# A two-layer hybrid decoder block on one core: the mixer's products turned feature-major, and one of four convolution chunks computed on GpSimd

## The chip, the cores and the metric

One core of one Trainium2 chip runs the whole program. The metric is the device time of one execution in microseconds; the time of the kernel before is the median of three executions.

## What is computed

The input is 256 tokens of 1024 features, all in float32, and there are two layers. The part that the change touches is the mixer, one of the four sublayers of a layer:

```python
def hybrid_mixer(u, w_in, b_f, w_attn_out, conv_w, conv_b, g_conv, w_conv_out, w_out):
    z = u @ w_in          # q | k | v | forget logits | conv GLU input | gate_attn | gate_conv
    y_attn = forgetting_attention(q, k, v, f_logit) @ w_attn_out
    y_conv = conformer_conv(z[..., C0:GA0], conv_w, conv_b, g_conv) @ w_conv_out
    merged = sigmoid(z[..., GA0:GC0]) * y_attn + sigmoid(z[..., GC0:]) * y_conv
    return merged @ w_out

def conformer_conv(glu_in, conv_w, conv_b, g_conv):
    a = glu_in[..., :512] * sigmoid(glu_in[..., 512:])
    y = depthwise_causal_conv(a, conv_w)      # 31 taps, 512 channels
    return silu(rmsnorm(y + conv_b, g_conv))
```

Here u is the RMS-normed input. Around the mixer stand, in each layer, a SwiGLU before it and one after it (1024 to 2816 and back) and a small gated embedding step.

## The kernel before, in words

**Products.** Every float32 operand of a product is split into a high and a low part, and each product is three matmuls: high by high, low by high, high by low. Activations are kept feature-major (`xs`, 128 features by 256 tokens for each of 8 chunks). Weights come from HBM in blocks of up to 1 MB into `raw` (3 buffers); ScalarE casts a half block of 1024 columns to `whi`, and VectorE computes `wlo = raw - whi` (6 buffers of each). Two forms of product exist. The feature-major form (`mm_b`) has the weights stationary and the 256 tokens moving, and gives 128 output features by 256 tokens. The token-major form (`mm_a`, used by `block_a`, lines 893 to 905) has 128 tokens stationary and 512 weight columns moving.

**The mixer** (line 908) uses the token-major form for the convolution's input, the values with the forget logits, the two gates, and the two output projections; queries and keys are feature-major (`heads`, line 1066). The root of the RMS norm is a factor for each token. In a token-major result it is one number for each partition, so ScalarE applies it as the `scale` of the tanh (`gate`, line 1187; `conv_in`, line 944). Where a token-major result is needed feature-major, TensorE transposes it: the convolution's input (4 transposes of 128x128 for each half, line 962 onward) and the merged result (16 of them, `turn` in `merged`, line 1220).

**The convolution** (`taps`, line 930) is 31 multiply-adds for each of four chunks of 128 channels by 256 tokens, all on VectorE, each `acc = abuf * w + acc`. They must be done before the norm of the convolution's result (`conv_end`, line 1044), which the products with `w_conv_out` wait for.

**GpSimd** issues a few DMAs, and in each mixer two: the running sum of the forget gates goes to HBM (`ncum`) and comes back spread over all partitions (`fb`). Two selects then put the causal mask into `fb` (`forget`, line 1005). VectorE's first step of every head of the attention reads `fb` (`sc`).

**Order.** All instructions are issued in an order that a planner in the program works out (class `Flow`, and `Weights` for the casts). It keeps a clock for TensorE, VectorE and ScalarE, with a fixed cost for each kind of step, and picks by priority. The taps have priority 4: they fill VectorE's time where a weight half is ready for 1 to 2 halves ahead of TensorE, and come after the next halves that TensorE needs. On the chip each engine runs its list strictly in that order. Nearly every instruction goes through the helper at line 304, so the profile gives L304 for it and groups are told apart by tile names.

Of the kernel before, what the change touches and what calls it, by code (L numbers as in the profile page):

```python
# [8 lines left out]
F32 = mybir.dt.float32  # L9
# [8 lines left out]
P = 128  # L18
T = 256
# [26 lines left out]
GAPS = 31, 62  # L46
# [405 lines left out]
def trunk(ctx: ExitStack, tc: tile.TileContext, x, p, g_ff1, w_ff1_in, w_ff1_out, g_mix, w_in, b_f,  # L452
# [3 lines left out]
    tensor, vector, scalar = (Pinned(tc, e) for e in (nc.tensor, nc.vector, nc.scalar))  # L456
# [52 lines left out]
    def a_blocks(src, kn, c0):  # L509
        order.extend(((src, k0, 4, c0, 512), None) for k0 in range(0, kn, 4))  # L510

    KPARTS = [(0, 8), (8, 7), (15, 7)]
    for l in range(L):
        W = w_in[l]
        ffn_blocks(w_ff1_in[l], w_ff1_out[l], l == 0)
        a_blocks(W, KD, (C0, C0 + CC))
        order.extend(((W, k0, 4, V0, AW + H), None) for k0 in range(0, KD, 4))
        a_blocks(W, KD, (C0 + 2 * P, C0 + CC + 2 * P))
        order.extend(((W, 0, KD, c, 2 * P), None) for c in (Q0, Q0 + 2 * P, K0, K0 + 2 * P))
        for c in (GA0, GA0 + 512, GC0, GC0 + 512):  # L520
            a_blocks(W, KD, c)
        for w in (w_attn_out[l], w_conv_out[l]):
            for n in range(2):
                a_blocks(w, KC, n * 512)
# [368 lines left out]
    def block_a(src, xs, kn, c0, needs):  # L893

        banks = [flow.take(mms) for _ in range(TT)]
        for k0 in range(0, kn, 4):
            blk = wts.take(src, k0, 4, c0, 512)
            for tt in range(TT):
                for h in blk.halves:
                    piece(mm_a_, MA, [(blk, k, (banks[tt].t, xs[k0 + k], tt), (k0 + k == 0, k0 + k == kn - 1))  # L900
                                      for k in range(h.a, h.b)], [needs[k0 + k] for k in range(h.a, h.b)])
            wts.release(blk)
        return banks

    def mm_a_(ps, xs, tt, w, start, stop):
        mm_a(ps, xs, tt, w, start, stop)

    def mixer(l, norm, nxt):
        W = w_in[l]
        norm.root()  # L910
        with tc.tile_pool(name="mixer", bufs=1) as ph, tc.tile_pool(name="attn", bufs=2) as at:
# [9 lines left out]
            scaled = {}  # L921

            def scales():
                yield norm.tok
                for name, f in (("half", 0.5),):
                    scaled[name] = small.tile([P, TT], F32, name=f"r{name}")
                    yield V, vc(TT), lambda: vector.tensor_scalar(out=scaled[name], in0=norm.rtok, scalar1=f, scalar2=None, op0=ALU.mult)
            have_scales = spawn(scales(), prio=0)

            def taps(cc):  # L930
                for t in range(TAPS):
                    for c in cc:
# [9 lines left out]
                        yield V, vc(T, 1), go  # L942

            def conv_in(banks, cc):

                yield have_scales
                rh = scaled["half"]
                avs = []
                for tt in range(TT):
                    sg = yield t1s  # L950
                    av = yield t2s
                    yield A, ac(T, 1), lambda: scalar.activation(out=sg.t[:, :T], in_=banks[tt].t[:, T:], func=AF.Tanh, scale=rh[:, tt:tt + 1])
                    yield A, ac(T, 1), lambda: scalar.activation(out=av.t[:, :T], in_=banks[tt].t[:, :T], func=AF.Copy, scale=rh[:, tt:tt + 1])
                    banks[tt].free()
                    yield V, vc(T), lambda: vector.scalar_tensor_tensor(out=av.t[:, :T], in0=sg.t[:, :T], scalar=1.0, in1=av.t[:, :T],
                                                                        op0=ALU.add, op1=ALU.mult)
                    sg.free()
                    avs.append(av)
                xp = yield xps
                pt = xp.t.rearrange("p (c t) -> p c t", c=2)  # L960

                def go():
                    for tt, av in enumerate(avs):
                        for i in range(2):
                            tensor.transpose(out=pt[:, i, tt * P:(tt + 1) * P], in_=av.t[:, i * P:(i + 1) * P], identity=ident)
                yield PE, 430, go
                for av in avs:
                    av.free()
                yield A, ac(2 * T), lambda: scalar.copy(out=abuf[:, cc[0]:cc[1] + 1, TAPS - 1:], in_=pt)
                xp.free()  # L970
# [3 lines left out]
            banks = block_a(W, norm.xs, KD, (C0, C0 + CC), norm.ready)  # L974
            in0 = spawn(conv_in(banks, (0, 1)))
# [29 lines left out]
            def forget():  # L1005
# [23 lines left out]
                nc.gpsimd.dma_start(out=rows, in_=ncum)  # L1029
                nc.gpsimd.dma_start(out=fb[1], in_=rows.partition_broadcast(P))  # L1030
                for dst, src in ((fb[0], fb[1][:, :, :P]), (fb[1][:, :, P:], fb[1][:, :, P:])):
                    nc.gpsimd.affine_select(out=dst, in_=src, pattern=[[0, H], [-1, P]], compare_op=ALU.is_ge, fill=NEG, base=0,
                                            channel_multiplier=1)
                have_f.at = flow.now + 16000
            spawn(forget(), prio=2)

            banks = block_a(W, norm.xs, KD, (C0 + 2 * P, C0 + CC + 2 * P), norm.ready)
            in1 = spawn(conv_in(banks, (2, 3)))
# [27 lines left out]
            def heads(c0, dst, scale):  # L1066
                evs = []
                for mm in range(AW // (2 * P)):
                    bank = flow.take(mms)
                    blk = wts.take(W, 0, KD, c0 + mm * 2 * P, 2 * P)  # L1070
                    for m in range(2):
                        for h in blk.halves:
                            ks = range(h.a, h.b)
                            piece(mm_b, MB, items_b(blk, bank, m, 0, ks, KD, norm.xs), [norm.ready[k] for k in ks])
                    wts.release(blk)
# [109 lines left out]
            sig = ph.tile([P, 2, TT, D], F32, name="sig")  # L1185

            def gate(banks, gi, cols):
                rh = scaled["half"]
                for tt in range(TT):
                    yield A, ac(512, 1), lambda: scalar.activation(out=sig[:, gi, tt, cols], in_=banks[tt].t, func=AF.Tanh, scale=rh[:, tt:tt + 1])  # L1190
                    banks[tt].free()
            gated = []
            for i in range(4):
                gi, n = divmod(i, 2)
                banks = block_a(W, norm.xs, KD, (GA0, GC0)[gi] + n * 512, norm.ready)
                gated.append(spawn(gate(banks, gi, slice(n * 512, (n + 1) * 512))))
# [11 lines left out]
            def ya_in(banks, n):  # L1208
                cols = slice(n * 512, (n + 1) * 512)
                yield gated[n]  # L1210
                for tt in range(TT):
                    yield V, vc(512), lambda: vector.scalar_tensor_tensor(out=sig[:, 0, tt, cols], in0=sig[:, 0, tt, cols], scalar=1.0, in1=banks[tt].t,
                                                                          op0=ALU.add, op1=ALU.mult)
                    banks[tt].free()
            have_ya = []
            for n in range(2):
                banks = block_a(w_attn_out[l], os_, KC, n * 512, os_ready)
                have_ya.append(spawn(ya_in(banks, n)))

            def merged(bank, n, tt):  # L1220
                cols = slice(n * 512, (n + 1) * 512)
                kk = slice(n * 4, n * 4 + 4)
                yield gated[2 + n]
                yield have_ya[n]
                m2 = yield t2s
                yield V, vc(512, 1), lambda: vector.scalar_tensor_tensor(out=m2.t, in0=sig[:, 1, tt, cols], scalar=1.0, in1=bank.t,
                                                                         op0=ALU.add, op1=ALU.mult)
                bank.free()
                yield V, vc(512), lambda: vector.tensor_tensor(out=m2.t, in0=m2.t, in1=sig[:, 0, tt, cols], op=ALU.add)
                xp = yield xps  # L1230
# [8 lines left out]
                xp.free()  # L1239

# [194 lines left out]
```

## Time and profile before

| | |
|---|---|
| median of three executions | 1121.93 us (1121.37 to 1122.11) |
| the profiled execution, its own time | 1121.54 us |
| its span, first to last instruction | 1119.5 us |
| TensorE busy | 1110.0 us (99%) |
| VectorE busy | 830.3 us (74%) |
| ScalarE busy | 600.4 us (54%) |
| GpSimd busy | 24.7 us (2%) |

The profile is one execution taken by the hardware profiler. Busy time of TensorE is that of overlapping matmuls, so the pace of its work is read from the start times of successive instructions, not from their lengths. Times in the trace count from the start of the span. The first mixer runs from about 195.5 to 331 us and the second from about 744 to 880 us.

### The profile page before, as it was taken

To read this page: it belongs to the slowest core of one execution; us is meant where nothing else is said; L and a number is where in the kernel's file an instruction comes from. 1 tells how busy PE (TensorE), PEld (TensorE's weight loads), DVE (VectorE), ACT (ScalarE), POOL (GpSimd) and SP (SyncE) were. 2 spreads that over 40 slices of the span, in tenths; PEclk is the share of its full clock that TensorE was granted. 3 is DMA by queue.
4 is the path that set the end of the run, shared out by engine and by line. 5 is a ranking of instruction groups with operands and counts; after the bars stand their busy time and mean duration, and the time that the engine had idled before them with its cause. 6 is when DMAs were issued, how large, how long until landed. Compare 5 with 4: busy or idle time off the path is not lost.

```text
span 1119.5 us, 21305 instructions
## 1 busy us (share of the span) xinstructions
PE 1110.0 (99%) x8900; PEld 1065.2 (95%) x8900; DVE 830.3 (74%) x1296; ACT 600.4 (54%) x874; POOL 24.7 (2%) x27
## 2 busy tenths in 40 slices
PE   9999999999999999999999999999999999999997
PEld 9999999897789999999999999999878999999996
DVE  7766656899997866656896665569999887665665
ACT  6544454558555544444654444457576555444454
POOL 1000000030000000000000000000200000000000
PEclk9999999999999999999999999999999999999998
DMA  9755566464457555565467555655535666555541
GB/s 306 227 181 196 170 203 195 150 225 152 157 166 251 183 194 189 174 207 202 144 206 231 184 187 178 208 190 186 174 131 163 216 194 222 194 185 190 190 152 39
DMA packets 188992, 209.77 MB, mean 187 GB/s; under 512 B 4056, under 2 KB 173120, under 8 KB 188640
## 3 DMA queue, kind: packets, MB, share of 16 engines
q1 hardware_dynamic: 188064, 205.60, 56.1%
q0 software_dynamic: 800, 2.80, 0.7%
q8 instruction: 70, 1.15, 0.4%
q14 instruction: 26, 0.21, 0.1%
q10 hardware_dynamic: 32, 0.01, 0.0%
HBM read 207.33 MB, written 1.06 MB: 186 GB/s over the span
## 4 chain that ended last, share of the span: by engine, by line
PE 98%; ACT 0%; DMA 0%; DVE 0%; issue 0%; SPq 0%; DVEq 0%; ACTq 0%
PE mmps L304 89%; PE xps L304 9%; DMA xin<-in_x_dram 0%; DVE sgate L304 0%; ACT sgate L304 0%; ACT sq L304 0%; DVE hT L304 0%; ACT L304 0%; SPq L381 0%; ACT xs L304 0%; DVE o L304 0%; DVEq L1430 0%; SPq L494 0%; DVE sqsum L304 0%; DVE rtok L304 0%
## 5 line engine op out<-in xcount | busy, mean ns | idle before, releaser
L304 DVE TENSOR_TENSOR wlo<-raw,whi 128x1024 fp32r<-128x1024 f32 (+3 forms) x400 | 473.2, 1195 | 201.2 <-ACT whi L304 154.8
L304 PE MATMUL mmps<-xs,whi 128*128 128x256 f32 x3456 | 594.5, 278 | 0.0
L304 ACT CAST whi<-raw 128x1024 fp32r<-128x1024 f32 (+3 forms) x400 | 404.9, 1021 | 345.1 <-PE mmps L304 283.5
L304 PEld LDWEIGHTS mmps<-xs,whi 128*128 128x128 f32 x3456 | 522.7, 188 | 0.5
L304 PE MATMUL mmps<-xs,wlo 128*128 128x256 f32 x1728 | 478.8, 277 | 0.0
L304 PEld LDWEIGHTS mmps<-xs,wlo 128*128 128x128 f32 x1728 | 325.1, 188 | 0.0
L304 PE MATMUL mmps<-whi,xs 128*128 128x512 f32 (+2 forms) x640 | 193.2, 377 | 0.0
L304 PE MATMUL mmps<-gs,whi 128*128 128x256 f32 x1056 | 179.7, 276 | 0.0
L304 PEld LDWEIGHTS mmps<-gs,whi 128*128 128x128 f32 x1056 | 158.9, 188 | 0.0
L304 PE MATMUL mmps<-gs,wlo 128*128 128x256 f32 x528 | 145.9, 276 | 0.0
L304 PEld LDWEIGHTS mmps<-whi,xs 128*128 128x128 f32 x640 | 116.2, 188 | 23.9 <-issue 3.4
L304 PE MATMUL mmps<-wlo,xs 128*128 128x512 f32 (+1 forms) x320 | 118.8, 371 | 0.0
L304 DVE SCALAR_TENSOR_TENSOR acc<-abuf,cols_taps,acc 128x256 f32<-128x256 f32 x240 | 99.3, 477 | 0.0
L304 PEld LDWEIGHTS mmps<-gs,wlo 128*128 128x128 f32 x528 | 99.1, 188 | 0.0
L304 PEld LDWEIGHTS mmps<-wlo,xs 128*128 128x128 f32 x320 | 60.3, 188 | 9.6
L304 PE MATMUL xps<-gs,whi 128*128 128x256 f32 x352 | 60.0, 276 | 0.0
L304 ACT CAST gs<-a 128x512 fp32r<-128x512 f32 x44 | 27.4, 623 | 53.3 <-DVE a L304 53.3
L304 PEld LDWEIGHTS xps<-gs,whi 128*128 128x128 f32 x352 | 53.0, 188 | 0.0
L304 PE MATMUL xps<-gs,wlo 128*128 128x256 f32 x176 | 48.6, 276 | 0.0
L304 ACT ACTIVATE xs<-hT,cols_mix 128x256 fp32r<-128x256 f32 (+1 forms) x56 | 28.2, 505 | 27.1 <-DVE hT L304 27.1
L304 DVE SCALAR_TENSOR_TENSOR hT<-mmps,hT 128x512 f32<-128x512 f32 x18 | 12.4, 691 | 32.9 <-PE mmps L304 32.8
L304 DVE TENSOR_TENSOR a<-a,mmps 128x512 f32<-128x512 f32 x44 | 30.3, 688 | 4.2
(138 smaller groups left out, 692.7 us busy)
## 6 DMA issues: line engine op xcount, KB each, us to landing
raw<-in_w_ff_in_dram SPq DMA_DIRECT2D x80, 1024.0 KB, 5.1
raw<-in_w_ff_out_dram SPq DMA_DIRECT2D x32, 896.0 KB, 4.8
raw<-in_w_in_dram SPq DMA_DIRECT2D x24, 1024.0 KB, 5.1
raw<-in_w_ff_out_dram SPq DMA_DIRECT2D x16, 1024.0 KB, 5.1
raw<-in_w_in_dram SPq DMA_DIRECT2D x16, 512.0 KB, 4.5
raw<-in_w_out_dram SPq DMA_DIRECT2D x16, 512.0 KB, 3.4
raw<-in_w_ple_gate_dram SPq DMA_DIRECT2D x8, 1024.0 KB, 5.2
raw<-in_w_ff_in_dram SPq DMA_DIRECT2D x12, 512.0 KB, 4.4
```

The source lines that it names most:

```text
L304: return self.tc.keep_in_program_order(f(*a, **k))
```

## The change

The mixer's products all take the feature-major form, but for the values and forget logits. `block_a` goes; `block_b` takes its place for the second half of the convolution's input, for queries and keys, gates and both output projections, and the first half of the convolution's input is written out in place. The transposes of the convolution's input and of the merged result go. Since a token now lies along the free dimension, the root is multiplied in by VectorE, from `norm.rall`, the root spread over all partitions (which the kernel before has too, for queries and keys). And the taps of chunk 0 are computed on GpSimd, each as a product and an add. The weight blocks are cut to suit: those of the gates have 8 chunks of 256 columns where they had 4 of 512.

```diff
+    def block_b(src, c0, xs, kn, needs):
+        bank = flow.take(mms)
+        blk = wts.take(src, 0, kn, c0, 2 * P)
+        for m in range(2):
+            for h in blk.halves:
+                ks = range(h.a, h.b)
+                piece(mm_b, MB, items_b(blk, bank, m, 0, ks, kn, xs), [needs[k] for k in ks])
+        wts.release(blk)
+        return bank
...
+            prods = slots(2, at, [P, T], "prod")
+            def taps_0(c=0):
+                for t in range(TAPS):
+                    src, w = abuf[:, c, t:t + T], gain(f"taps{l}", t, c, KC)
+                    if t == 0:
+                        gpsimd.tensor_scalar(out=acc[:, c], in0=src, scalar1=w, scalar2=gain("conv_b", l, c, KC), op0=ALU.mult, op1=ALU.add)
+                    else:
+                        h = yield prods
+                        gpsimd.tensor_scalar(out=h.t, in0=src, scalar1=w, scalar2=None, op0=ALU.mult)
+                        gpsimd.tensor_tensor(out=acc[:, c], in0=acc[:, c], in1=h.t, op=ALU.add)
+                        h.free()
+                    yield flow.now + 1700
...
-                        yield V, vc(T, 1), go
...
+                        if c:
+                            yield V, vc(T, 1), go
...
+            def conv_in(av, bv, cc):
+                yield norm.all
+                r = bc(norm.rall, 2)
+                sg = yield t1s
+                yield V, vc(2 * T), lambda: vector.tensor_tensor(out=sg.t, in0=chunks(bv), in1=r, op=ALU.mult)
+                bv.free()
+                yield A, ac(2 * T), lambda: scalar.activation(out=sg.t, in_=sg.t, func=AF.Tanh, scale=0.5)
+                a = yield t2s
+                yield V, vc(2 * T), lambda: vector.scalar_tensor_tensor(out=a.t, in0=chunks(av), scalar=0.5, in1=r, op0=ALU.mult, op1=ALU.mult)
+                av.free()
+                yield V, vc(2 * T), lambda: vector.scalar_tensor_tensor(out=abuf[:, cc[0]:cc[1] + 1, TAPS - 1:], in0=sg.t, scalar=1.0, in1=a.t,
                                                                         op0=ALU.add, op1=ALU.mult)
...
-                nc.gpsimd.dma_start(out=rows, in_=ncum)
-                nc.gpsimd.dma_start(out=fb[1], in_=rows.partition_broadcast(P))
+                gpsimd.dma_start(out=rows, in_=ncum)
+                yield flow.now + 1500
+                gpsimd.dma_start(out=fb[1], in_=rows.partition_broadcast(P))
+                yield flow.now + 6500
...
+            def gate(bank, z):
+                yield norm.all
+                yield V, vc(2 * T), lambda: vector.tensor_tensor(out=z, in0=chunks(bank), in1=bc(norm.rall, 2), op=ALU.mult)
+                bank.free()
+                yield A, ac(2 * T), lambda: scalar.activation(out=z, in_=z, func=AF.Tanh, scale=0.5)
...
-                xp = yield xps
-
-                def turn():
-                    for c in range(4):
-                        tensor.transpose(out=xp.t[:, c * P:(c + 1) * P], in_=m2.t[:, c * P:(c + 1) * P], identity=ident)
-                yield PE, 430, turn
-                m2.free()
-                yield from split([x[:, :, tt * P:(tt + 1) * P] for x in ms[kk]],
-                                 xp.t.rearrange("p (c t) -> p c t", c=4), 512)
+                yield from split(ms[kk], m2, 2 * T)
```

How the lists of instructions move is shown at two places. The first is GpSimd's list in the first mixer, from the clearing of `abuf` (the convolution's input, with its margin of 30 zeros) on. Before:

```order
L918 MEMSET abuf 128x4x30
L1029 DMA ncum<-fc 8x256
L1030 DMA fb_2357<-ncum 128x2048
L1032 AFFINE_SELECT fb_2356<-fb_2357 128x1024
L1032 AFFINE_SELECT fb_2357<-fb_2357 128x8x128
L1275 DMA pin<-in_p_dram 128x2x256
```

In the changed kernel, from the tenth tap (`prod` and `acc` are a tap's product and its sum, `abuf` the convolution's input):

```order
L304 TENSOR_SCALAR prod_2789<-abuf_2359,cols_taps0_141 128x256
L304 TENSOR_TENSOR acc_2361<-acc_2361,prod_2789 128x256
L304 DMA ncum_2795<-fc_2666 8x256
L304 TENSOR_SCALAR prod_2811<-abuf_2359,cols_taps0_141 128x256
L304 TENSOR_TENSOR acc_2361<-acc_2361,prod_2811 128x256
L304 DMA fb1_2358<-ncum_2795 128x2048
L304 TENSOR_SCALAR prod_2834<-abuf_2359,cols_taps0_141 128x256
```

The same list where the mask is made:

```order
L304 TENSOR_SCALAR prod_2895<-abuf_2359,cols_taps0_141 128x256
L304 TENSOR_TENSOR acc_2361<-acc_2361,prod_2895 128x256
L304 AFFINE_SELECT fb0_2357<-fb1_2358 128x1024
L304 AFFINE_SELECT fb1_2358<-fb1_2358 128x8x128
L304 TENSOR_SCALAR prod_2918<-abuf_2359,cols_taps0_141 128x256
```

The first DMA now stands behind 10 of the 31 taps, the second behind 11, and the selects behind 14; the other 17 taps follow the selects.

The second place is VectorE's list where the first half of the convolution's input is made and the taps begin (`t` are the factors of the gated input, `wlo` the low halves of weights). Before:

```order
L304 SCALAR_TENSOR_TENSOR t_2467<-t_2466,t_2467 128x256
L304 TENSOR_TENSOR wlo<-raw,whi 128x1024
L304 SCALAR_TENSOR_TENSOR t_2490<-t_2489,t_2490 128x256
L304 TENSOR_TENSOR wlo<-raw,whi 128x1024
L304 TENSOR_SCALAR acc<-abuf,cols_taps_141,cols_mix 128x256 x2
L304 SCALAR_TENSOR_TENSOR acc<-abuf,cols_taps_141,acc 128x256 x15
L304 TENSOR_TENSOR wlo<-raw,whi 128x1024
```

In the changed kernel:

```order
L304 TENSOR_TENSOR t_2512<-mmps,rall 128x512
L304 TENSOR_TENSOR wlo<-raw,whi 128x1024
L304 SCALAR_TENSOR_TENSOR t_2533<-mmps,rall 128x512
L304 SCALAR_TENSOR_TENSOR abuf<-t_2512,t_2533 128x2x256
L304 TENSOR_SCALAR acc<-abuf,cols_taps_141,cols_mix 128x256
L304 SCALAR_TENSOR_TENSOR acc<-abuf,cols_taps_141,acc 128x256 x8
L304 TENSOR_TENSOR wlo<-raw,whi 128x1024
```

Two of the three steps that make the input now read PSUM (`mmps`), the third writes `abuf` directly, and of the first two chunks' taps only one chunk's are left on VectorE.

## Rows read from the trace of the kernel before

**Rows 1.** The page: TensorE's share of the span, and the chain that ended last, by engine

```profile
PE 1110.0 (99%) x8900; PEld 1065.2 (95%) x8900; DVE 830.3 (74%) x1296; ACT 600.4 (54%) x874; POOL 24.7 (2%) x27
...
PE 98%; ACT 0%; DMA 0%; DVE 0%; issue 0%; SPq 0%; DVEq 0%; ACTq 0%
```

**Rows 2.** Busy time of the engines in the first mixer and in two stretches of it

```profile
core 0: us, PE busy (x) PEld busy (x) DVE busy (x) ACT busy (x) POOL busy (x), PEclk, DMA share, GB/s
...
195.50:331.00 135.50, 135.50 (x803) 114.41 (x803) 127.33 (x271) 85.07 (x151) 9.22 (x5) 1.00 0.50 167
...
208.50:253.60 45.10, 45.10 (x328) 41.56 (x327) 45.08 (x84) 25.32 (x34) 8.76 (x4) 1.00 0.53 181
...
253.60:303.70 50.10, 50.10 (x256) 38.27 (x255) 49.04 (x124) 35.55 (x82) 0.00 (x0) 1.00 0.44 149
```

**Rows 3.** TensorE in order of time, both forms: start us, us, engine, line, operation

```profile
216.63 0.39 PE L304 MATMUL mmps<-wlo,xs 128*128 128x512 f32 x1
...
225.62 0.40 PE L304 MATMUL mmps<-wlo,xs 128*128 128x512 f32 x1
...
226.33 0.28 PE L304 MATMUL mmps<-xs,wlo 128*128 128x256 f32 x1
...
229.73 0.28 PE L304 MATMUL mmps<-xs,wlo 128*128 128x256 f32 x1
```

**Rows 4.** TensorE's groups of instructions, whole kernel (count behind the x)

```profile
L304 PE MATMUL mmps<-wlo,xs 128*128 128x512 f32 x256 | 100.7, 393 | 0.0
...
L304 PE MATMUL xps<-ident,t 128*128 128x128 f32 x48 | 6.5, 273 | 0.0
```

**Rows 5.** TensorE in order of time around the transposes

```profile
206.58 0.28 PE L304 MATMUL mmps<-wlo,xs 128*128 128x256 f32 x1
...
206.94 0.28 PE L304 MATMUL mmps<-wlo,xs 128*128 128x264 f32 x1
...
207.75 0.28 PE L304 MATMUL mmps<-wlo,xs 128*128 128x256 f32 x1
...
323.58 0.40 PE L304 MATMUL mmps<-wlo,xs 128*128 128x512 f32 x1
...
325.16 0.40 PE L304 MATMUL mmps<-wlo,xs 128*128 128x512 f32 x1
```

**Rows 6.** VectorE in order of time, ahead of the attention

```profile
241.92 2.85 DVE L304 SCALAR_TENSOR_TENSOR acc<-abuf,cols_taps,acc 128x256 f32<-128x256 f32 x7
244.69 0.68 DVE L304 SCALAR_TENSOR_TENSOR KA<-mmps,rall 128x512 f32<-128x512 f32 x1
245.29 2.35 DVE L304 TENSOR_TENSOR wlo<-raw,whi 128x1024 fp32r<-128x1024 f32 x2
247.56 2.46 DVE L304 SCALAR_TENSOR_TENSOR acc<-abuf,cols_taps,acc 128x256 f32<-128x256 f32 x6
```

**Rows 7.** GpSimd in order of time, setup and first mixer

```profile
2.04 0.31 POOL masks.py:199 TENSOR_SCALAR_AFFINE_SELECT ident<-ident 128x128 f32<-128x128 f32 x1
...
224.62 0.52 POOL L1029 DMA_DIRECT2D ncum<-fc  x1 [33.29 <-ACT fc L304]
...
233.26 7.65 POOL L1032 TENSOR_SCALAR_AFFINE_SELECT fb<-fb 128x1024 f32<-128x1024 f32 x2 [6.10 <-DMA fb<-ncum]
```

**Rows 8.** VectorE in order of time beside GpSimd's two selects

```profile
233.22 2.34 DVE L304 TENSOR_TENSOR wlo<-raw,whi 128x1024 fp32r<-128x1024 f32 x2
235.48 2.45 DVE L304 SCALAR_TENSOR_TENSOR acc<-abuf,cols_taps,acc 128x256 f32<-128x256 f32 x6
237.86 0.67 DVE L304 SCALAR_TENSOR_TENSOR QA<-mmps,rall 128x512 f32<-128x512 f32 x1
238.46 3.53 DVE L304 TENSOR_TENSOR wlo<-raw,whi 128x1024 fp32r<-128x1024 f32 x2
```

**Rows 9.** TensorE at 248.6 us, and VectorE's first step of the attention

```profile
248.59 0.39 PE L304 MATMUL mmps<-wlo,xs 128*128 128x512 f32 x1
...
253.59 0.28 DVE L304 CUSTOM_DVE_ANT_0 sc<-xps,fb 128x128 f32<-128x128 f32 x1
```

More of the change, by code (lines that the diff above doesn't have):

```diff
@@ L45 @@
 WLEN = 1024 + 2 * LINE
-GAPS = 31, 62
+GAPS = 32, 62
 WARM = (6, 3, 0, 0, 0)
@@ L455, in trunk @@
     nc = tc.nc
-    tensor, vector, scalar = (Pinned(tc, e) for e in (nc.tensor, nc.vector, nc.scalar))
+    tensor, vector, scalar, gpsimd = (Pinned(tc, e) for e in (nc.tensor, nc.vector, nc.scalar, nc.gpsimd))
     flow = Flow()
@@ L891, in ffn @@
                     spawn(residual(chunks(hs[0]), hs[0].free, 2 * mm, 2, 0.5, nxt))
[L893 to L906, printed above, removed]
+    def block_b(src, c0, xs, kn, needs):
[7 more added lines that the diff above has]
+        return bank
     def mixer(l, norm, nxt):
@@ L920, in mixer @@
             t1s, t2s = slots(2, at, [P, 512], "t1"), slots(2, at, [P, 512], "t2")
[L921 to L928, printed above, removed]
+            prods = slots(2, at, [P, T], "prod")
[10 more added lines that the diff above has]
+                    yield flow.now + 1700
             def taps(cc):
+                done = spawn(taps_0(), at=flow.now) if 0 in cc else None
                 for t in range(TAPS):
@@ L1068, in heads @@
                 for mm in range(AW // (2 * P)):
[L1069 to L1075, printed above, removed]
+                    bank = block_b(W, c0 + mm * 2 * P, norm.xs, KD, norm.ready)
                     evs.append(spawn(heads_out(bank, dst[:, 2 * mm:2 * mm + 2], scale)))
@@ L1182, in mixer @@
                 spawn(attention(j))
[L1185 to L1196, printed above, removed]
+            sig = ph.tile([P, 2, KD, T], F32, name="sig")
+            def gate(bank, z):
[3 more added lines that the diff above has]
+                yield A, ac(2 * T), lambda: scalar.activation(out=z, in_=z, func=AF.Tanh, scale=0.5)
+            gated = [[spawn(gate(block_b(W, g + mm * 2 * P, norm.xs, KD, norm.ready), sig[:, i, 2 * mm:2 * mm + 2])) for mm in range(KD // 2)]
+                     for i, g in enumerate((GA0, GC0))]
             def silu_table():
@@ L1206, in mixer @@
             ms = parts(xsp, KD, "xs")
[L1208 to L1215, printed above, removed]
@@ L1241, in mixer, with ya_in @@
-            ms_ready = []
-            for n in range(2):
-                banks = block_a(w_conv_out[l], cs, KC, n * 512, cs_ready)
-                ms_ready.append([spawn(merged(banks[tt], n, tt), prio=0) for tt in range(TT)])
+            def ya_in(bank, mm):
+                y = sig[:, 0, 2 * mm:2 * mm + 2]
+                yield gated[0][mm]
+                yield V, vc(2 * T), lambda: vector.scalar_tensor_tensor(out=y, in0=y, scalar=1.0, in1=chunks(bank), op0=ALU.add, op1=ALU.mult)
+                bank.free()
@@ new lines, in mixer, with merged @@
+            have_ya = [spawn(ya_in(block_b(w_attn_out[l], mm * 2 * P, os_, KC, os_ready), mm)) for mm in range(KD // 2)]
+            def merged(bank, mm):
+                kk = slice(2 * mm, 2 * mm + 2)
+                yield gated[1][mm]
+                yield have_ya[mm]
+                h = yield t2s
+                m2 = h.t.rearrange("p (m t) -> p m t", m=2)
+                yield V, vc(2 * T), lambda: vector.scalar_tensor_tensor(out=m2, in0=sig[:, 1, kk], scalar=1.0, in1=chunks(bank), op0=ALU.add, op1=ALU.mult)
+                bank.free()
+                yield V, vc(2 * T), lambda: vector.tensor_tensor(out=m2, in0=m2, in1=sig[:, 0, kk], op=ALU.add)
+                yield from split(ms[kk], m2, 2 * T)
+                h.free()
@@ L1246, in w_out_part @@
+            ms_ready = [[], []]
+            for mm in range(KD // 2):
+                ms_ready[mm // 2].append(spawn(merged(block_b(w_conv_out[l], mm * 2 * P, cs, KC, cs_ready), mm), prio=0))
             def w_out_part(hs, mm, k0, done=None):
```

74 lines of the change are left out of this document (20 added, 54 removed).

## The prediction

> **What bounds the kernel now.** The page comes first: TensorE is busy for 99% of the span, and the chain that ended last is TensorE's for 98% [rows 1]. So a gain is TensorE work removed, and a loss is a stall of TensorE that does not exist today. Next, the busy times by stretch [rows 2]: in the first mixer TensorE is busy for all 135.5 us, and VectorE for 127.33 of them; between its first tap and its first step of the attention VectorE is busy for 45.08 of 45.10 us. It feeds TensorE there with `wlo`, so the question is how far ahead it is. The first of the two `wlo` casts that begin at 245.29 ends half-way through their 2.35 us, at 246.5 [rows 6]; TensorE reads it at 248.59 [rows 9]. VectorE leads by 2.1 us. The last view is of what VectorE and GpSimd do to each other [rows 7, 8].
>
> The profiled execution took 1121.54 us, 0.4 under the median of 1121.93; I work out changes on its rows and put them on the median.
>
> **TensorE: 8.3 us removed.** In the token-major form thirteen groups of three 512-wide matmuls lie between 216.63 and 225.62, 0.692 us each [rows 3]. In the feature-major form ten groups of three 256-wide ones lie between 226.33 and 229.73, 0.340 each, so 0.680 for the same arithmetic. There are 256 token-major groups (one `wlo` matmul each) [rows 4]: 256 x 0.012 = 2.9 us. The 48 transposes [rows 4] go too. Around four of the convolution's, successive `wlo` matmuls of the values are 0.81 us apart (206.94 to 207.75) where 0.36 is usual; around eight of the merge's the distance is 1.58 (323.58 to 325.16) where 0.69 is usual [rows 5, 3]. That is 0.45 and 0.89, each twice in a layer: 2.7 a layer, 5.4 in all. With nothing else, 1121.9 - 8.3 = 1113.6.
>
> **VectorE's own work: less by 5.5 us a layer.** Seven taps take 241.92 to 244.69, 0.396 each; a 512-wide product with a PSUM input takes 0.60 [rows 6]. Off go 31 taps, 12.3 us. On come 8 gate products (4.8) and 6 steps of 0.60 for the convolution's input in place of 4 about as wide as a tap (2.0). That leaves 121.8 us for a mixer of some 131, which fits. But the saving is not where VectorE is tight. Ahead of its first step of the attention the new list has 56 taps and 15 casts where the old had 60 and 14: 1.6 us less and 1.1 more, and about 1 us more for the convolution's second half. The stretch holds 45 us of work again. Behind it 27 taps fewer (10.7 us) meet 6 gate products (3.6), so 7 us come free in those 50.
>
> ScalarE loses its scaled copies, the weight bytes are the same, and the merge needs no PSUM bank for transposes. I put these at nothing: TensorE's work covers them, ScalarE being busy for 85 of 135.5 us, and DMA for half of their time [rows 2]. Should raw weights come late once, with the projections' blocks halved to 512 KB, I allow 1 us either way.
>
> **GpSimd: the unknown.** It runs 61 instructions a layer, in the tight stretch above all. The trace has one case beside VectorE, the two selects of 1024 elements from 233.26 on, 7.65 us for both [rows 7], while one of 128 elements on an idle chip took 0.31. VectorE's two casts from 238.46 took 3.53 us where two others beside the same selects took 2.34 [rows 8]: the selects cost it 1.19 us. Part of their work fell on the `QA` step (0.60 on VectorE), which reads PSUM and one SBUF tensor and kept its length; so they held VectorE's way to SBUF for up to 1.19 + 0.60 = 1.8 us, 0.87 ns an element. A tap's product on 256 elements, one input, then holds it for 0.22 us. Its add reads two tensors: not less than 0.22, and at most 0.45 if they are read in turn. So a tap costs VectorE 0.45 to 0.67 us where both want the way, and 31 taps 14 to 21 us. About a sixth falls on VectorE's PSUM reads (7 of them in the tight stretch, more in the attention) and costs nothing: 11.6 to 17.3. The lead absorbs 2.1: 9.5 to 15.2 us a layer is the stall of TensorE, since what VectorE loses there it cannot make good before TensorE needs the next half. GpSimd's own pace lets most taps fall there: two instructions of at least 0.31 and two waits for half an instruction of VectorE (0.2 to 0.57) make 1.0 to 1.8 us a tap, 31 to 55 us for all, in a stretch of 45 that grows as it is slowed. I take 11 us a layer, nearer to the low end, because the only row is of an instruction with one input. **Forecast: 1113.6 + 22 = 1136 us.**
>
> A rule weighed against this, first by the rows: a select was issued at 233.26 while a cast was under way, and VectorE's next eight instructions, up to the end of the `QA` step, were no longer than elsewhere [rows 7, 8]; the selects cost VectorE time only afterwards. The Trainium skill (SBUF — State Buffer, section "Who interferes with whom") says that a VectorE instruction with two SBUF inputs contends with a GpSimd instruction that reads SBUF, and that the second to issue waits until the first has finished. On the contention the trace agrees (1.19 us lost); on the wait it does not, since the select waited for more than the one cast in progress. By that rule GpSimd gets in after each instruction of VectorE, which is the forecast's case, 1136; by the row it can be kept out, which is the first rival below. The Trainium skill's GPSIMD Engine Reference (section "Elementwise — side-by-side cycle accounting") gives 4497 ns for an add of 2048 elements; by that an add of 256 is an estimated 0.56 us, a tap 0.78, and the sum would come to about 1149. No run here shows it, and the forecast does not use it.
>
> **The rivals.**
> *GpSimd waits, and the mask is late.* For: from 233.22 to 237.86 VectorE ran two casts and six taps at their usual lengths (2.34, and 2.45 as against 2.46) with a select pending [rows 8, 6]; GpSimd got nowhere between instructions that read two SBUF tensors. If each tap needs an instruction of VectorE that reads less, the new list has nine such places ahead of the attention's first step. `ncum`'s DMA stands behind ten taps, so it is issued at about 254 and not at 224.62; the selects could start 8.6 us after it (224.62 to 233.26) [rows 7], so the mask is there at about 264.5, 11 us after VectorE wants it (253.59) [rows 9]. VectorE stands still, and TensorE after its lead: 9 us a layer, 18 in all, 1131.6. Against: the second select did get in between two casts, or they would not have been long.
> *Faster.* GpSimd's small reads fall on VectorE's PSUM steps and pauses, or are too short to matter, and the lag stays near the lead. It decides at 8.3 / 2 = 4.2 us of stall a layer. With only the 14 taps ahead of the selects in the tight stretch, at 0.45, VectorE lags by 6.3, less 0.9 for PSUM reads and 2.1 of lead: 3.3 a layer, 1120. With no hold at all, 1113.6. For: GpSimd's shortest instruction is 0.31 us, and VectorE gets 7 us back behind the attention's first step. Against: rows 8.
> *The change does not do what it says* is excluded: the lists show the transposes gone and 61 GpSimd instructions a layer.
>
> **Chances.** About 0.2% of this kernel's time, 2.2 us, is what a measurement can tell from no change. VectorE held by GpSimd, 1132 to 1144: 0.36. The mask late, 1126 to 1135: 0.22. Little stall, 1113 to 1119.7: 0.34. Between, where the stall cancels the gain: 0.08. So slower 0.58, same 0.08, faster 0.34. The likeliest single case has the range 1132 to 1144; since cases of both signs hold much of the chance, the range that should hold 8 in 10 reaches from 1113 to 1146, the upper end with 1 us a layer beyond the bound.
>
> **What would show it right or wrong.** Right on TensorE: groups of three at 0.34 us throughout the mixers but for the values, and no `ident,t` transposes. Right on the loss: `wlo` casts and taps of VectorE that last longer than 1.17 and 0.41 us in the first 50 us of each mixer, and idle time of TensorE there that ends on `wlo`; about 11 us more in that stretch. For the first rival: casts of usual length, GpSimd products of several us, the first `sc` step late and waiting for `fb`. Wrong: mixers that shorten by 4 us each, with no idle time of TensorE.

## The result, and the profile after

The changed kernel takes 1149.91 us (median of four runs, 1148.89 to 1150.76) against 1121.65 for the kernel before on the same chip: a ratio of 1.025, 95% interval 1.0238 to 1.0262, 28.3 us slower. Its profiled execution took 1149.98. The forecast was 1136 with a range to 1146: the direction is right, the size is not.

The page of the changed kernel, first the busy times and the granted clock by slices, then the chain that ended last, then three of the costliest groups (busy us, mean ns of one, idle time ahead):

```profile
PE 1116.4 (97%) x9620; PEld 1105.3 (96%) x9620; DVE 852.4 (74%) x1252; ACT 595.1 (52%) x858; POOL 157.0 (14%) x149
...
PEclk9999999988999999999999999999999999999999
...
PE 82%; DVE 15%; ACT 1%; issue 1%; DMA 1%; SPq 0%; DVEq 0%; ACTq 0%
...
L304 DVE SCALAR_TENSOR_TENSOR acc<-abuf,cols_taps,acc 128x256 f32<-128x256 f32 x180 | 102.8, 607 | 1.7
...
L304 POOL TENSOR_SCALAR prod<-abuf,cols_taps 128x256 f32<-128x256 f32 x60 | 83.1, 1384 | 0.2
...
L304 POOL TENSOR_TENSOR acc<-acc,prod 128x256 f32<-128x256 f32 x60 | 55.7, 928 | 5.0
```

Where the chain was TensorE's for 98% [rows 1] it is now VectorE's for 15%. VectorE executes 44 instructions fewer and is busy 22 us longer. Its taps take 607 ns on the mean, and a GpSimd tap 1.38 + 0.93 us. The granted clock, 9 tenths or more in every slice but the last before the change, is 8 in two slices of the first mixer.

The place is read from two landmarks on TensorE, the spread of `rtok` (the root of a norm, for each token) at a mixer's start and the next one behind that layer's feed-forward block. In order of time, the changed kernel:

```profile
199.87 0.60 PE L304 MATMUL xps<-ident,rtok 128*128 128x128 f32 x4
...
558.17 0.60 PE L304 MATMUL xps<-ident,rtok 128*128 128x128 f32 x4
...
762.37 0.60 PE L304 MATMUL xps<-ident,rtok 128*128 128x128 f32 x4
...
1120.05 0.60 PE L304 MATMUL xps<-ident,rtok 128*128 128x128 f32 x4
```

The two stretches are 358.30 and 357.68 us long. In the kernel before they were 344.51 and 344.49 (198.27 to 542.78, 747.04 to 1091.53). So 27.0 us are lost in the two mixers, 13.8 and 13.2, and 1.6 ahead of the first one, where the first transposes wait longer for the input. That start differs by a us or more between the runs below and is not followed up.

What TensorE waited for in the first mixer, 195 to 345 us (total, times, longest):

```profile
PE mmps L304 <- DVE wlo L304: 6.0, 3, 3.9
PE xps L304 <- DVE nm L304: 3.5, 1, 3.5
PE xps L304 <- DVE csq L304: 0.4, 1, 0.4
```

These are the waits on `wlo` that the prediction named, and one for VectorE at the second pair of heads' scores. Before the change there were none. The largest, in order of time on TensorE, and VectorE beside it:

```profile
226.83 0.28 PE L304 MATMUL mmps<-xs,wlo 128*128 128x256 f32 x1
...
227.17 0.28 PE L304 MATMUL mmps<-xs,wlo 128*128 128x256 f32 x1
...
227.63 0.39 PE L304 MATMUL mmps<-xs,whi 128*128 128x256 f32 x2
231.97 0.58 PE L304 MATMUL mmps<-xs,wlo 128*128 128x256 f32 x1 [3.95 <-DVE wlo L304]
```

```profile
226.44 2.49 DVE L304 SCALAR_TENSOR_TENSOR acc<-abuf,cols_taps,acc 128x256 f32<-128x256 f32 x4
228.86 0.94 DVE L304 TENSOR_TENSOR fl<-fl,fe 8x256 f32<-8x256 f32 x1
229.72 0.47 DVE L304 SCALAR_TENSOR_TENSOR acc<-abuf,cols_taps,acc 128x256 f32<-128x256 f32 x1
230.12 0.67 DVE L304 TENSOR_TENSOR_SCAN fe<-ones,fl 8x256 f32<-8x256 f32 x1
230.72 2.32 DVE L304 TENSOR_TENSOR wlo<-raw,whi 128x1024 fp32r<-128x1024 f32 x2
```

TensorE's groups of three are 0.34 us apart up to the wait (226.83 to 227.17), as in [rows 3]. VectorE is busy all the time and late. The casts here keep their length (1.2 us each); it is the taps ahead of them that have grown.

### The profile page after: what moved, and what is told of

The parts are those of the page before. It is cut to its first block, busy times and chain, and to the rows that moved or that the text cites. A ratio compares the mean times of both kernels' runs of the same rounds, so it can differ in the third digit from the quotient of the medians.

```text
span 1148.2 us, 22821 instructions
## 1 busy us (share of the span) xinstructions
PE 1116.4 (97%) x9620; PEld 1105.3 (96%) x9620; DVE 852.4 (74%) x1252; ACT 595.1 (52%) x858; POOL 157.0 (14%) x149
## 4 chain that ended last, share of the span: by engine, by line
PE 82%; DVE 15%; ACT 1%; issue 1%; DMA 1%; SPq 0%; DVEq 0%; ACTq 0%
PE mmps L304 74%; PE xps L304 8%; DVE acc L304 7%; DVE wlo L304 5%; DMA xin<-in_x_dram 1%; ACT sc L304 0%; DVE sig L304 0%; DVE sc L304 0%; DVE t L304 0%; DVE xs L304 0%; DVE fl L304 0%; DVE abuf L304 0%; DVE QA L304 0%; ACT L304 0%; DVE csq L304 0%
## 5 line engine op out<-in xcount | busy, mean ns | idle before, releaser
L304 PE MATMUL mmps<-xs,whi 128*128 128x256 f32 x4480 | 782.3, 280 | 0.0
L304 PEld LDWEIGHTS mmps<-xs,whi 128*128 128x128 f32 x4480 | 683.8, 190 | 4.9 <-issue 3.4
L304 PE MATMUL mmps<-xs,wlo 128*128 128x256 f32 x2240 | 624.7, 279 | 13.5 <-DVE wlo L304 13.3
L304 PEld LDWEIGHTS mmps<-xs,wlo 128*128 128x128 f32 x2240 | 425.0, 190 | 15.1 <-DVE wlo L304 15.1
L304 DVE SCALAR_TENSOR_TENSOR acc<-abuf,cols_taps,acc 128x256 f32<-128x256 f32 x180 | 102.8, 607 | 1.7
L304 POOL TENSOR_SCALAR prod<-abuf,cols_taps 128x256 f32<-128x256 f32 x60 | 83.1, 1384 | 0.2
L304 POOL TENSOR_TENSOR acc<-acc,prod 128x256 f32<-128x256 f32 x60 | 55.7, 928 | 5.0
L304 DVE SCALAR_TENSOR_TENSOR hT<-mmps,hT 128x512 f32<-128x512 f32 x18 | 12.4, 689 | 32.1 <-PE mmps L304 32.1
L304 PEld LDWEIGHTS xps<-gs,wlo 128*128 128x128 f32 x176 | 33.0, 188 | 0.0
```

The source lines that it names most:

```text
L304: return self.tc.keep_in_program_order(f(*a, **k))
```

## The experiments

**Who pays: all taps on VectorE.** The changed kernel without `taps_0`, the taps of chunk 0 (the first quarter) on VectorE again:

```diff
-                done = spawn(taps_0(), at=flow.now) if 0 in cc else None
...
-                        if c:
-                            yield V, vc(T, 1), go
...
+                        yield V, vc(T, 1), go
```

> The changed kernel with all four chunks' taps on VectorE, as in the kernel before; GpSimd keeps only its DMAs and selects. Theory (GpSimd's reads of SBUF hold VectorE up, and TensorE stalls and drops its clock behind that): TensorE's gain of 8.3 us stays and the stalls go: 1114 to 1118 us, with the casts at 1.2 us again. Rival (the root's products on VectorE are the load that makes the casts late; GpSimd only took work away): with 12.3 us more a mixer on VectorE it is slower than the changed kernel, over 1150.

1141.44 us (ratio 1.0177, 1.016 to 1.0194): neither. The waits in the first 60 us of a mixer are gone, but others stand at the convolution's end, here in the first mixer:

```profile
PE xps L304 <- DVE csq L304: 4.2, 1, 4.2
PE xps L304 <- DVE rtok L304: 2.5, 1, 2.5
PE mmps L304 <- ACT xs L304: 2.2, 1, 2.2
PE mmps L304 <- DVE xs L304: 0.7, 1, 0.7
```

They follow one another on the way from the last tap to the first `xs` of the convolution's output. So without GpSimd the new list is too long for VectorE: TensorE waits some 10 us a layer, and the landmarks are 353.70 and 354.78 us apart. Still it is 8.5 us faster than the changed kernel, though VectorE does 31 taps a layer more.

**The taps alone, in the kernel before.** Chunk 0's taps on GpSimd, with the changed kernel's spacing of the forget gates' DMAs, and nothing else of the change:

```diff
+                done = spawn(taps_0(), at=flow.now) if 0 in cc else None
...
-                        yield V, vc(T, 1), go
+                        if c:
+                            yield V, vc(T, 1), go
```

> The kernel before with one edit, the taps of chunk 0 on GpSimd (with the changed kernel's spacing of the forget gates' DMAs); its products stay token-major. Theory: GpSimd's taps alone cost what the change lost, 28 us and the 8.3 us that TensorE's gain hid: 1148 to 1160. Rival: with VectorE relieved of 31 taps a layer it is as fast as before or faster, 1118 to 1123.

1158.32 us (one execution), 36.5 over the kernel before, as expected: the taps' move costs more than the whole change, the rest of which gives some of it back. Chunk 1's taps stand alone on VectorE here too, so this run does not tell GpSimd's hold from what the runs without its taps find below.

**Reads or the engine's mere presence.** Two kernels like the one with all taps on VectorE. In the first GpSimd adds 61 memsets a mixer, which only write; in the second it repeats chunk 0's taps into a tile that nobody reads. Both are extra work that the output doesn't use. The edit of the first:

```diff
+                    gpsimd.memset(sp[:, :T], 0.0)
+                    if t:
+                        gpsimd.memset(sp, 0.0)
```

> The kernel of e1 with 61 more instructions a mixer on GpSimd, in the places that the taps had, that only write: memsets of 256 and 512 elements into a tile that nothing reads. The other engines' lists are those of e1. Theory (it is reads that hold VectorE): within 2 us of e1, casts and taps at their usual lengths. Rival (any GpSimd instruction beside VectorE holds it, or delays the mask): slower than e1 by 15 us or more.

> The kernel of e1 with GpSimd computing chunk 0's taps once more into a tile that nothing uses, so the same 61 reading instructions as in the changed kernel, while VectorE does all four chunks. The other engines' lists are those of e1. Theory: the reads alone bring the loss back, 25 to 50 us over e1. Rival (what costs is that something waits for GpSimd's result): within 3 us of e1.

1142.24 and 1175.29 us (one execution each) against 1141.44: 0.8 us for the writes, 33.9 for the reads, both as expected. Nothing holds the memsets back, so 19 of the first mixer's 61 had run before the first tap; 34 run in a row later. These, and seven taps of VectorE beside them:

```profile
237.81 16.19 POOL L304 MEMSET sp<- 128x256 f32 x34
```

```profile
242.12 2.86 DVE L304 SCALAR_TENSOR_TENSOR acc<-abuf,cols_taps,acc 128x256 f32<-128x256 f32 x7
```

Seven taps beside GpSimd's products and adds, in the second kernel:

```profile
208.14 4.49 DVE L304 SCALAR_TENSOR_TENSOR acc<-abuf,cols_taps,acc 128x256 f32<-128x256 f32 x7
```

Beside an idle GpSimd seven take 2.85 [rows 6]. That only GpSimd's reads of SBUF hold a VectorE instruction with two SBUF inputs, and its writes do not, is what the Trainium skill says (SBUF — State Buffer, "Who interferes with whom"); these rows agree, 2.86 us beside writes and 4.49 beside reads.

**The change without GpSimd's taps.** GpSimd does tap 0 of chunk 0 only, and nobody does the other 30, so the convolution lacks them. The lists of the other engines are those of the changed kernel.

```diff
-                    else:
-                        h = yield prods
-                        gpsimd.tensor_scalar(out=h.t, in0=src, scalar1=w, scalar2=None, op0=ALU.mult)
-                        gpsimd.tensor_tensor(out=acc[:, c], in0=acc[:, c], in1=h.t, op=ALU.add)
-                        h.free()
```

> The changed kernel with only tap 0 of the convolution's first quarter on GpSimd; the other 30 taps of that quarter are left out altogether. The instructions of TensorE, VectorE and ScalarE are those of the changed kernel. Theory (TensorE's work is 8 us less, and all of the loss is GpSimd's reads beside VectorE): 1112 to 1116 us, no stall of TensorE over 1 us in either mixer, granted clock at the full level in both, 34 to 38 us under the changed kernel. Rival (part of the loss is VectorE's own new list, the six steps of the convolution's input and the gate products): 1120 us or more, with waits for wlo left in the first 60 us of a mixer.

1122.96 us (1.0003 to 1.0023): the rival. Without those 30 taps there is still nothing of the 8 us that TensorE was to gain. TensorE waits for `wlo` (1.0 us) and at the scores (1.4) in the first mixer. The landmarks are 344.74 us apart in both layers: 13.6 and 12.9 less than in the changed kernel, which is the part of GpSimd's 30 taps, and 4.4 more than the 340.4 that TensorE's work alone would need. VectorE's list explains them; the first taps in this kernel, then those of the kernel with all taps on VectorE:

```profile
208.77 3.09 DVE L304 SCALAR_TENSOR_TENSOR acc<-abuf,cols_taps,acc 128x256 f32<-128x256 f32 x6
211.78 1.22 DVE L304 TENSOR_TENSOR wlo<-raw,whi 128x1024 fp32r<-128x1024 f32 x1
```

```profile
207.65 2.85 DVE L304 SCALAR_TENSOR_TENSOR acc<-abuf,cols_taps,acc 128x256 f32<-128x256 f32 x7
210.42 1.22 DVE L304 TENSOR_TENSOR wlo<-raw,whi 128x1024 fp32r<-128x1024 f32 x1
```

Seven taps in 2.77 us, 0.396 each, where they alternate between the sums of chunks 0 and 1; six in 3.01 where all go into chunk 1's sum. There the records of the trace are 0.52 us apart from start to start: an instruction that needs the result of the one just ahead starts 0.04 us after its end, and one that doesn't need it some 0.08 before (here only the cast behind the six starts early, hence 3.01). With chunk 0 gone, chunk 1's 31 taps stand alone: 31 x 0.125 = 3.9 us a layer. (The price of 0.83 us a tap in some expectations held three of these waits, 0.38, which are not GpSimd's.)

**Two sums for chunk 1.** The last kernel (30 taps of chunk 0 not done), with the odd taps of chunk 1 in a tile of their own, added at the end:

```diff
+                                a = odd if c == 1 and t % 2 else acc[:, c]
...
+                    yield V, vc(T), lambda: vector.tensor_tensor(out=acc[:, 1], in0=acc[:, 1], in1=odd, op=ALU.add)
```

> As the run with one tap on GpSimd (30 taps of the first quarter left out), but VectorE sums the odd taps of the second quarter in a tile of their own and adds it at the end, so that no tap follows one on the same sum. Theory (with the first quarter gone from VectorE, 31 taps on one sum stand one behind another, 0.52 us apart instead of 0.40, and these 31 x 0.125 = 3.9 us a layer, less 0.4 for the added sum, are its stall of 3.6 a layer): 1114.5 to 1117.5 us, and waits of TensorE for wlo and at the scores under 0.5 us. Rival (the stall is the order of VectorE's list or the selects): 1121 to 1124 us, the same waits.

1116.03 us (ratio 0.9945, 0.9931 to 0.996), as expected: the view of waits names none for TensorE in the first mixer, and the landmarks are 341.29 and 341.22 us apart (199.85 to 541.14, 745.34 to 1086.56). So waiting for its own sum cost VectorE, and by it TensorE, 3.5 us a layer; and TensorE's gain is there, 3.2 us a layer of the 4.15 worked out.

**The same in the whole change.** All taps done, chunk 1's on two sums:

> The changed kernel, complete, with the second quarter's taps on two sums. Theory (3.5 us a layer of VectorE come off in the tight stretch, and the granted clock falls for a shorter time): 1138 to 1144 us. Rival (VectorE and GpSimd share SBUF so that what VectorE no longer waits for its own sum it waits for GpSimd): 1147 to 1151 us, with VectorE's cycle of three taps to one of GpSimd's still 2.0 us long.

1146.63 us (1.0201 to 1.0232), between the two and nearer to the rival: 3.3 us less than the changed kernel, not 7. VectorE and GpSimd in order of time:

```profile
209.65 0.96 DVE L304 SCALAR_TENSOR_TENSOR odd<-abuf,cols_taps,odd 128x256 f32<-128x256 f32 x1
210.53 0.70 DVE L304 SCALAR_TENSOR_TENSOR acc<-abuf,cols_taps,acc 128x256 f32<-128x256 f32 x1
211.15 0.47 DVE L304 SCALAR_TENSOR_TENSOR odd<-abuf,cols_taps,odd 128x256 f32<-128x256 f32 x1
211.55 0.95 DVE L304 SCALAR_TENSOR_TENSOR acc<-abuf,cols_taps,acc 128x256 f32<-128x256 f32 x1
```

```profile
208.42 1.09 POOL L304 TENSOR_SCALAR prod<-abuf,cols_taps 128x256 f32<-128x256 f32 x1
209.59 0.74 POOL L304 TENSOR_TENSOR acc<-acc,prod 128x256 f32<-128x256 f32 x1
210.31 1.09 POOL L304 TENSOR_SCALAR prod<-abuf,cols_taps 128x256 f32<-128x256 f32 x1
```

Three VectorE taps go by for one of GpSimd's, from 209.65 to 211.55: 1.90 us where 3 x 0.396 = 1.19 would do. A GpSimd tap costs VectorE 0.71 us here. In the changed kernel, GpSimd again:

```profile
208.80 1.09 POOL L304 TENSOR_SCALAR prod<-abuf,cols_taps 128x256 f32<-128x256 f32 x1
209.97 0.85 POOL L304 TENSOR_TENSOR acc<-acc,prod 128x256 f32<-128x256 f32 x1
210.81 1.08 POOL L304 TENSOR_SCALAR prod<-abuf,cols_taps 128x256 f32<-128x256 f32 x1
```

Here the cycle is 2.01 us, and three taps on one sum need 3 x 0.52 = 1.56 by themselves, so the price is 0.45. GpSimd gets in partly where VectorE waits for its own sum; the two losses overlap.

**The clock.** After TensorE's longer waits the granted clock fell to half (the 1.2 GHz level; 0.50 from 270 to 275 us). Windows of the changed kernel: the first mixer, and two stretches that hold a wait (busy us of PE, PEld, DVE, ACT, POOL, then the granted clock, DMA share, GB/s):

```profile
199.00:331.00 132.00, 122.05 (x991) 117.09 (x990) 122.29 (x222) 72.63 (x133) 75.06 (x65) 0.95 0.45 145
227.50:240.00 12.50, 8.55 (x50) 8.36 (x49) 12.17 (x18) 7.12 (x8) 10.06 (x11) 0.73 0.52 182
262.00:276.00 14.00, 10.55 (x64) 9.37 (x64) 13.61 (x35) 6.70 (x25) 13.50 (x13) 0.76 0.44 145
```

To see what that costs, TensorE was given matmuls of zeros, added to its running sums just where it had waited:

```diff
+        for _ in range(fill[0]):
+            tensor.matmul(out=ps, lhsT=zero, rhs=xs[0], start=False, stop=False)
```

> The changed kernel, complete, with matmuls of zeros added to the running sums of TensorE just where it stalls (96 and 96 in the two mixers, of 256 columns, 0.113 us each), so that it is busy there. Theory (the granted clock falls to half because TensorE stood still, and after the last stall of a mixer that costs 3.4 us in the first and 1.7 to 3.4 in the second; before the last stall VectorE sets the pace and the clock costs nothing): granted clock at the full level through both mixers, 1142 to 1146 us. Rival one (every us at the half level costs half a us): 1136 to 1140 us. Rival two (the clock falls all the same, or the matmuls come in the way): 1149 to 1153 us.

1148.55 us (1.022 to 1.0254). The same windows of this kernel:

```profile
199.00:331.00 132.00, 128.87 (x1094) 123.97 (x1093) 121.79 (x219) 71.16 (x131) 74.51 (x65) 1.00 0.45 144
227.50:240.00 12.50, 12.12 (x106) 11.91 (x105) 12.25 (x18) 8.12 (x9) 10.12 (x10) 1.00 0.62 213
262.00:276.00 14.00, 14.00 (x120) 12.72 (x120) 13.60 (x38) 8.21 (x28) 13.50 (x13) 1.00 0.36 111
```

The clock stays at its full level (2.4 GHz), and almost nothing comes of it: the landmarks are 358.18 and 357.78 us apart, against 358.30 and 357.68. The 1.4 us that the total is shorter are the start (198.32 against 199.87 at the first landmark). All three expectations miss; rival two is nearest, but the clock did not fall. Its other reason, the matmuls in the way, holds in part: counted from the first landmark, TensorE went on from the third row of zeros at 61.0 us, without a wait, where it had gone on from its wait at 59.4. From the second pair of heads' scores to the third it then took 4.5 us in place of 7.7. TensorE at the convolution's sum of squares (`csq`), in the changed kernel and in this one:

```profile
307.76 0.58 PE L304 MATMUL xps<-ones,csq 128*128 128x1 f32 x4 [0.43 <-DVE csq L304]
```

```profile
305.65 0.58 PE L304 MATMUL xps<-ones,csq 128*128 128x1 f32 x4 [0.66 <-DVE csq L304]
```

That is 107.9 and 107.3 us behind the landmark, and in both kernels TensorE waits for VectorE there. What a faster TensorE gains behind a wait is lost again where VectorE is the one that is late. By the Trainium skill (TensorE: Matmul & The Clock Gate, "Terms") the penalty is about the throttled time times the share of the clock that is lost; that would be an estimated 0.05 x 132 = 6.6 us in this mixer, and the run shows 0.1, with the zeros' own 1.6 in it.

**Parts of the change.** Gates and output projections feature-major, the convolution's input token-major, all taps on VectorE:

> Half of the change: gates and the two output projections feature-major, merge without transposes; the convolution's input stays token-major and all 124 taps stay on VectorE. Theory (VectorE has no room for 8 gate products of 0.60 us ahead of the sum of squares of the convolution, as the run with all taps on VectorE showed): stalls of some 9 us a layer at that sum, and TensorE 5.7 us shorter: 1130 to 1140 us. Rival (the lateness came from the convolution's input steps in the tight stretch, which this kernel does not have): 1116 to 1119 us.

1150.37 us (1.0237 to 1.0274), worse than the theory's range; the waits are where it put them, at the convolution's end (the first mixer: 3.1 for `xs`, 3.0 for `rtok`). Some 5 us of it lie ahead of the first mixer (first landmark at 203.48, before 198.27), which the run does not explain. And the other part alone:

> The other part alone: only the convolution's input is feature-major (no transposes of it, two VectorE steps more with the root); gates, outputs and merge as before, all taps on VectorE. TensorE's work: 0.9 us a layer of transposes and some 0.4 a layer of pace less, 2.6 in all. Theory (the 2.0 us a layer of VectorE are covered by its lead of 2.1): 1118.5 to 1120.5 us. Rival (the lead does not cover it, and a stall drops the clock): 1122 to 1130 us.

1123.96 us (1.0009 to 1.0027): the rival's number, by a little, but not its reason, since the granted clock stayed at 1.00 and TensorE's only wait over 0.3 us in the first mixer is 1.0 for `xs`, behind the convolution. The landmarks are 345.80 and 346.21 us apart, 1.3 and 1.7 more than before: VectorE's two steps more cost at least what TensorE saves, and its chain behind the convolution is late. Neither half pays without room on VectorE.

**GpSimd later.** The first 14 taps of chunk 0 on VectorE, the other 17 on GpSimd, all behind the mask's selects:

```diff
+                yield on_vector
+                yield masked
+                for t in range(NV, TAPS):
```

> The changed kernel with the first 14 taps of the first quarter on VectorE, and the other 17 on GpSimd, all of them behind the mask's selects; complete. Theory (a tap on GpSimd costs VectorE 0.83 us wherever it falls, more than the 0.40 it saves): the convolution ends later than with all taps on VectorE, 1148 to 1160 us. First rival (behind the selects many of VectorE's instructions read PSUM, a tap costs it about as much as it saves): 1136 to 1146 us. Second rival (there the reads cost nothing, and 17 taps of 0.40 come off): 1114 to 1124 us, which would beat the kernel before.

1133.69 us (1.0098 to 1.0125): between the two rivals, 16 us under the changed kernel and 8 under all taps on VectorE. The theory, with 0.83 us a tap, falls. What a tap costs behind the selects this run does not tell alone, since chunk 1 has 17 taps on one sum in it too.

**Help from ScalarE instead.** All taps done, none on GpSimd. For 35 of a layer's 62 pairs of taps ScalarE makes both products and VectorE adds them at once:

```diff
+                            scalar.activation(out=h.t[:, i], in_=abuf[:, c, t:t + T], func=AF.Copy, scale=gain(f"taps{l}", t, c, KC))
...
+                    yield V, vc(2 * T), lambda: vector.tensor_tensor(out=both, in0=both, in1=h.t, op=ALU.add)
```

> The changed kernel, complete, with no tap on GpSimd: VectorE does some taps as before, alternating between two sums, and for half of the taps of the first half of the convolution and two thirds of the second's ScalarE makes the two products (256 wide, Copy with the tap as its scale) and VectorE adds both with one 512-wide add of 0.60 us in place of two taps of 0.40. 35 of 62 pairs of taps go that way: 35 x 0.19 = 6.7 us a layer less for VectorE than with all taps on it; ScalarE does 70 products of some 0.35 more, 25 us. Theory (VectorE's work sets the time, and ScalarE does not hold it up as GpSimd does): the stall of 11 us a layer behind the convolution shrinks to 0 to 4, 1116 to 1122 us. Rival one (ScalarE's reads of SBUF hold VectorE as GpSimd's do): over 1135 us. Rival two (ScalarE is late with whi, so that wlo is late in the tight stretch): 1123 to 1132 us, with TensorE waiting for whi or wlo there.

1126.67 us (1123.64 to 1128.48; ratio 1.0027 to 1.0051), 23 us faster than the changed kernel and 0.4% slower than the one before. The theory's range misses, and the number lies in rival two's; but of rival two's sign little is there, 0.4 us of waits for `wlo` in the first mixer. Rival one is excluded: ScalarE reads SBUF for its products while three of VectorE's taps keep their 0.40 us each.

```profile
206.35 1.71 ACT L304 ACTIVATE prod<-abuf,cols_taps 128x256 f32<-128x256 f32 x4 [1.02 <-DVE abuf L304]
```

```profile
207.02 1.27 DVE L304 SCALAR_TENSOR_TENSOR acc<-abuf,cols_taps,acc 128x256 f32<-128x256 f32 x3
```

What is left in the first mixer, in the profiled execution, which was the fastest with 1123.64:

```profile
PE xps L304 <- DVE csq L304: 1.3, 1, 1.3
PE xps L304 <- DVE nm L304: 1.3, 1, 1.3
PE mmps L304 <- DVE wlo L304: 0.4, 2, 0.3
```

Two adds in a row on the same sums are 0.72 to 0.79 us apart and not 0.60; the reason found above accounts for 0.73 (an add's 0.69 and 0.04), the rest was not followed up. No version that does the whole convolution beat the kernel before.

## Why the prediction was wrong in size

By its own steps, a layer at a time: it had -4.15 us for TensorE and +11 for the stall, 6.9 in all; the landmarks show 13.8 and 13.2.

- *TensorE, 8.3 us removed.* Right in kind, and the transposes are gone. With no waits left (two sums, no GpSimd taps) 3.2 of the 4.15 us a layer show. The rest, 0.9, was not followed up.
- *"VectorE's own work": the step that failed.* "The stretch holds 45 us of work again" was worked out with 0.396 us for every tap, from [rows 6], where seven taps alternate between two sums. The change leaves chunk 1 alone on VectorE, and the list that stands ahead of the prediction shows it: one first tap and then eight of one sum, where there were two and then fifteen of two. On one sum a tap takes 0.52 us. That is 3.9 us a layer by the rows and 3.5 by the run with two sums. VectorE's lead, 2.1 us by [rows 6, 9], was gone before GpSimd did anything: without its 30 taps TensorE already waited for `wlo` and at the scores.
- *GpSimd's hold.* Right in kind, a little small. The bounds were 0.45 to 0.67 us a tap; the rows give 0.45 in the changed kernel and 0.71 where VectorE does not wait for itself. The stall that follows from GpSimd was put at 11 us a layer, within 9.5 to 15.2; it is 13.6 and 12.9. What had been taken off the hold, a sixth for PSUM reads and the lead, does not show: 13.6 / 30 taps is 0.45 each, the whole price by the changed kernel's rows. The loss fell on the taps; the casts, which were to last longer too, mostly kept 1.2 us, and three pairs took 2.67 to 3.24 in place of 2.35 (from 242.52, 257.63 and 264.55). The Trainium skill's rule that the second to issue waits (SBUF — State Buffer, "Who interferes with whom") stood for the forecast's case, and GpSimd did get in between the taps, once in 2.01 us.
- *Together* 3.5 + 13.2 in place of 11 is 5.7 us a layer more, and TensorE's 0.9 less gain makes 6.6. Twice that and the start's 1.6 are 14.8; between the profiled executions 28.4 us were measured where the sum had 13.7.
- *Luck.* The estimate of 0.78 us a tap that the prediction set aside came to about 1149, the measured time. It puts 18 us a layer on GpSimd, where 13.6 and 12.9 were measured, and nothing on VectorE's own sum.
- *The mask late*: excluded. The selects began at 242.55 and took 4.16 us, VectorE's first `sc` came only at 268.36, GpSimd was not starved, and TensorE's waits end on `wlo` and `nm`, not on the mask.
- *Faster*: it needed under 4.2 us of stall a layer. Even without GpSimd's taps the own order of VectorE's list cost 3.5.
- *ScalarE, DMA and the raw weights at nothing*: no wait of TensorE names them.
- *The clock*: the prediction left it out. Kept full by zeros, it changed the stretches by 0.1 us; what it would give without the zeros' own 1.6 us, no run shows.

## What to carry to other kernels

Work that is moved to an engine sharing a path with the bound one is not gone: here a tap on GpSimd saved VectorE 0.40 us and cost it 0.45 to 0.71, while with ScalarE's products the taps beside them kept 0.40. When a part is taken out of an engine's list, look at what now stands next to each other in it, since a duration read where instructions alternate does not hold where each needs the one before. And a lower granted clock behind a wait is a symptom before it is a cost: ask first whether TensorE is what the next wait waits for.

## What was not expected of the hardware

- VectorE's instructions overlap by some 80 ns, and that is lost when one needs its predecessor's result: 0.52 us against 0.396 for a 256-wide tap, 0.72 to 0.79 against 0.60 for a 512-wide add.
- GpSimd's price for VectorE depends on how VectorE runs: 0.45 us a tap where VectorE waits for its own sum, 0.71 where it does not.
- 98 and 96 matmuls of zeros in the two mixers kept the granted clock at its full level through waits that otherwise brought it to half, and the stretches changed by 0.1 us.
- Whether the half level has a price where TensorE is the bound behind the wait was not tried. With all taps on VectorE it seems to: the granted clock was 0.52 from 320 to 330 us, and the first stretch is 12.4 us longer than the 341.29 of the kernel without waits, of which the waits are 9.6.
